# A hybrid decoder layer: the FFN's up-projection by seven half-wide products, its activations through DRAM

## The chip, the cores and the metric

One Trainium2 chip, one core. The metric is the device time of one execution in microseconds (us), as the median of several runs. TensorE (PE) multiplies; VectorE (DVE), ScalarE (ACT) and GpSimd (POOL) do the elementwise work; SyncE (SP) issues the DMAs. On-chip memory (SBUF) has 128 partitions; products are accumulated in PSUM, in banks of 512 float32 columns.

## The reference

One layer (width 2048, 512 tokens, FFN width 5632) of a decoder with two parallel mixers, then an FFN:

```python
h = rms_norm(x, mix_norm_g)
p = h @ w_in                                  # split into a_val, a_gate, q, k, v, z, b, a
out_a = conformer_conv_group(a_val, a_gate, ...)
out_b = gated_deltanet_group(q, k, v, z, b, a, ...)
x = x + concat([out_a, out_b]) @ w_out        # 2048 x 2048
h = rms_norm(x, ffn_norm_g)
gate, up = split(h @ w_up, 2)                 # w_up 2048 x 11264
gate = causal_depthwise_conv(gate, ffn_conv_w) + ffn_conv_b     # width 3
x = x + (silu(gate) * up) @ w_down            # 5632 x 2048
return rms_norm(x, final_norm_g)
```

Everything is float32. The change lies in the last five lines.

## The kernel before

Everything is held transposed: channels in the 128 partitions, the 512 tokens along the free axis. A product is cut into output tiles of 128 channels; a tile needs one step per block of 128 input channels, called k here. TensorE multiplies a rounded float32 format, so both factors are split into a high and a low part and a step is three matmuls (`mm3`, line 470): high weights by high input, high weights by low input, low weights by high input, each 128x128 weights by 512 tokens into one bank. Each of the three loads its weights anew.

`mtile` (line 476) makes one output tile and `plan_all` (line 518) lists the weights in the order of use. `load_next` (line 438) brings them by SP's queue in tiles `wraw` of 1024 columns, three of them in flight; `split_piece` (line 448) makes pieces of 512 columns (four k): `whi` by a cast on ACT, `wlo` by a subtraction on DVE.

Order of the program: input projection with the two mixers between its tiles (operands `xgh`, `xgl`, 32 tiles of the pool that `A`, line 323, draws from); first half of the output projection (`obh`, `obl`), conformer's pointwise product (`yh`, `yl`, giving `ah`, `al`), second half of the output projection, whose result `x2` stays in SBUF and is split into `h2h`, `h2l` (16 pairs). Two pools hold these 16 pairs: `H2` (line 1245) puts the first 22 tiles (k 0 to 10) into `late`, on the left, and the last 10 (k 11 to 15) into `late2`, at the right end of the partition.

The FFN runs in four chunks of 11 of its 44 tiles. `ffn_tile` (line 1263) makes a gate tile by 16 k, times `rstd2` (the RMS factor of each token, made beside the first tile), the width-3 convolution, SiLU, times `rstd2` again; an up tile by 16 k, the product of the two, and its split into `acth`, `actl`. After each chunk `down` (line 1281) adds 16 tiles of 11 k each to `x2`. The last two tiles of the last chunk are made in token halves of 256 (`half_tiles`, line 494), so that the final norm of the first half runs beside the second.

A planner (`Flow`) writes every engine's order while the program is recorded: it keeps a clock per engine by assumed costs and places the elementwise steps between the matmuls. All instructions are issued by one helper, so they all stand under line 94; one goes by the tiles' names.

Of the kernel before, what the change touches and what calls it, by code (L numbers as in the profile page):

```python
# [31 lines left out]
CHUNKS = 4  # L32
FC = NF // CHUNKS
EPS = 1e-6
# [6 lines left out]
H2_LEFT = 22  # L41
SPLIT_TILES = 2
# [30 lines left out]
class Engine:  # L73
    """Emits an engine's instructions and keeps the engine's clock by their cost."""
# [24 lines left out]
class Flow:  # L99
    """Sets every engine's instruction order: steps of the dependent chains between the bulk products."""  # L100
# [37 lines left out]
    def key(self, ap):  # L138
        n = ap.tensor.name
        return n if not n.startswith(("scr_d", "scr_n", "scr_o", "scr_y", "x2")) else (n, ap.offset)  # L140

    def account(self, eng, op, out, ins, kw):
# [148 lines left out]
def S(*aps):  # L291
# [5 lines left out]
    "y1", "e1", "d2p", "y2p", "e2",  # L297
# [4 lines left out]
def tile_trunk(ctx: ExitStack, tc: tile.TileContext, xT, w_k, w_ba, w_m, pw, w_out, w_up, w_down, par_d, cst_d, out):  # L302
# [6 lines left out]
    apool = ctx.enter_context(tc.tile_pool(name="acts", bufs=1))  # L309
    cctx, gctx = ExitStack(), ExitStack()  # L310
# [12 lines left out]
    def A(name, dt=F32R):  # L323
        return fl.tile(apool, [P, T], dt, "a", 32, nm(name))
# [27 lines left out]
    def alloc(tag, name, shape):  # L352
        fl.live[tag] += 1
        if tag == "misc":
            t = misc(name)
        elif tag == "DE":
# [79 lines left out]
    nsplit = [0, 0]  # L436

    def load_next():
        i = len(raws)
        if i < len(plan):  # L440
# [7 lines left out]
    def split_piece():  # L448
        i, o = nsplit
        if i >= len(plan):  # L450
            return
        n, step = plan[i][1:]
        w = min(step, n - o)
        src = raws[i][:, o : o + w]
        if i >= len(plan) - 2 * SPLIT_TILES:
            hi, lo = L("whi", F32R, "h2", H2_LEFT), L("wlo", F32R, "h2", H2_LEFT)
# [19 lines left out]
    def mtile(xs, release=False):  # L476
# [3 lines left out]
        while k < n:  # L480
            hi, lo = pieces.popleft()
            step = split_piece()
            for j in range(min(4, n - k, 8 - k % 8)):
                sl = blk(j)
# [3 lines left out]
                if release:  # L488
                    fl.live["a"] -= 2
# [4 lines left out]
    def half_tiles(xs, tiles, kept, half):  # L494
        ts = slice(half * 256, (half + 1) * 256)
        n = len(xs)
        for m in range(tiles):
            ps = acc()
            for k in range(n):
# [5 lines left out]
                hi, lo = kept[m * 3 + k // 4]  # L505
# [12 lines left out]
    def plan_all():  # L518
# [4 lines left out]
        for m in range(KT):  # L523
# [3 lines left out]
        for m in range(KT):  # L527
            plan_tile(w_out[m][:, 1024:2048], 1024)
        for f in range(NF):
            plan_tile(w_up[2 * f], D)  # L530
            plan_tile(w_up[2 * f + 1], D)
            if f % FC == 0 and f:
                for m in range(KT):
                    plan_tile(w_down[f // FC - 1, m], FC * P)
        for m in range(KT):
            plan_tile(w_down[CHUNKS - 1, m], FC * P)

    def split_scaled(src, g, name, alloc):
        hi = alloc(name + "h", F32R)
        lo = alloc(name + "l", F32R)  # L540
# [4 lines left out]
    def split_plain(src, name):  # L545
        hi = A(name + "h")
        lo = A(name + "l")
# [45 lines left out]
    scr_o = dram.tile([NH, P, T], F32, name="scr_o")  # L593
    scr_s, scr_t, scr_e = [dram.tile([NH * NB, P, 32], F32, name=n) for n in ("scr_s", "scr_t", "scr_e")]
# [11 lines left out]
    plan_all()  # L606
    xts = []
# [29 lines left out]
    for k in range(KT):  # L637
# [4 lines left out]
        hi, lo = split_scaled(xs, mix_g[:, k : k + 1], "xg", A)  # L642
# [501 lines left out]
    def z_task(h, ps, scan_ev):  # L1144
# [13 lines left out]
        while fl.live["a"] > 2 * KT - 2 or (h > 0 and not z_ev[h - 1].done):  # L1158
# [10 lines left out]
    fl.live["a"] = 2 * KT  # L1169

    def in_tile():
        left[0] -= 1
        return mtile(xg, left[0] == 0)
# [31 lines left out]
    late = ctx.enter_context(tc.tile_pool(name="late", bufs=1, reuse_waits="tile"))  # L1205

    def L(name, dt=F32, tag="lt", bufs=4):
        return fl.tile(late, [P, T], dt, tag, bufs, nm(name))

# [11 lines left out]
    x2, x2g = [], []  # L1221
    for m in range(KT):
        if m % 4 == 0:
            x2g.append(late.tile([P, 4, T], F32, tag="x2", bufs=KT // 4, name=nm("x2")))
        t = x2g[m // 4][:, m % 4, :]
# [4 lines left out]
        x2.append(t)  # L1230
    fl.drain(y_ev)
    ahl = []
    for m in range(NC):
# [6 lines left out]
        ahl.append((hi, lo))  # L1240
    cctx.close()
# [166 lines left out]
```

## Time and profile before

| | us |
|---|---|
| median of 3 runs | 2234.42 (2234.21 to 2236.41) |
| profiled execution, first to last instruction | 2233.0 |
| PE busy | 2219.0 (99%) |
| weight loads busy (beside PE) | 1832.2 (82%) |
| DVE busy | 1185.1 (53%) |
| ACT busy | 775.0 (35%) |
| DMA, mean over the span | 106 GB/s |

The profiled execution's span is 2233.0 us; the median of the runs shown lies 1.4 us above it. Matmuls are pipelined: one is shown from its start to its modelled end, which is longer than the distance to the next start, so a matmul's cost in a stream is read from the distance between starts. DVE's and ACT's instructions overlap their neighbours a little too. In a row of instructions by group the figures after the bar are the group's busy time, the mean length of one, and the idle time of that engine just before them, with what ended it.

### The profile page before, as it was taken

The numbers are of one execution on the slowest core, as the hardware profiler recorded it, in microseconds if no ns is written. First come the engines' busy times: TensorE is split into PE (matmuls) and PEld (weight loads), VectorE is DVE, ScalarE is ACT, GpSimd is POOL, SyncE is SP. The second block draws the span as 40 slices with busy tenths as digits, with TensorE's granted clock in tenths as the row PEclk, the third lists the DMA queues.
The fourth block names the chain that finished last, engine by engine and source line by source line (L and its number), as shares of the span: only waits on it lengthen the run. The fifth ranks groups of instructions, "written<-read, shape, count | busy, mean of one in ns | idle before, by whom it ended". The sixth has DMA issues, their size and how long they took to land.

```text
span 2233.0 us, 26443 instructions
## 1 busy us (share of the span) xinstructions
PE 2219.0 (99%) x10172; PEld 1832.2 (82%) x10172; DVE 1185.1 (53%) x2037; ACT 775.0 (35%) x1336; POOL 59.5 (3%) x59
## 2 busy tenths in 40 slices
PE   9999999999999999999999999999999999999997
PEld 7888888888888888888888888888888888888887
DVE  6899778888735544444334444334444333444444
ACT  5633554344323433322222323222233222233332
POOL 0310100000000000000000000000000000000000
PEclk9999999999999999999999999999999999999999
DMA  5352423233532222222332222332232233222223
GB/s 193 99 165 95 123 95 117 95 114 129 180 122 95 95 95 95 95 94 93 95 101 101 97 99 85 98 99 96 94 100 89 97 101 105 95 95 95 93 92 118
DMA packets 99438, 236.28 MB, mean 106 GB/s; under 512 B 21360, under 2 KB 42224, under 8 KB 99312
## 3 DMA queue, kind: packets, MB, share of 16 engines
q1 hardware_dynamic: 99168, 234.59, 31.8%
q8 instruction: 79, 1.29, 0.2%
q14 instruction: 47, 0.39, 0.1%
q10 hardware_dynamic: 144, 0.01, 0.0%
HBM read 220.41 MB, written 14.16 MB: 105 GB/s over the span
## 4 chain that ended last, share of the span: by engine, by line
PE 99%; issue 0%; DVE 0%; DMA 0%; SPq 0%; ACT 0%; POOLq 0%; POOL 0%; DVEq 0%
PE acc L94 94%; PE tr L94 1%; PE e L94 1%; PE pv L94 0%; PE ba L94 0%; PE po L94 0%; PE y L94 0%; PE psn L94 0%; PE pk L94 0%; PE pq L94 0%; DVE x L94 0%; PE y2p L94 0%; DMA wraw<-in_w_k_dram 0%; PE dec L94 0%; PE qk L94 0%
## 5 line engine op out<-in xcount | busy, mean ns | idle before, releaser
L94 DVE TENSOR_TENSOR wlo<-wraw,whi 128x512 fp32r<-128x512 f32 (+1 forms) x788 | 527.4, 678 | 557.5 <-ACT whi L94 551.6
L94 ACT CAST whi<-wraw 128x512 fp32r<-128x512 f32 (+1 forms) x788 | 473.2, 608 | 830.0 <-PE acc L94 784.8
L94 PE MATMUL acc<-h2h,whi 128*128 128x512 f32 x1408 | 551.3, 392 | 0.0
L94 PE MATMUL acc<-h2l,whi 128*128 128x512 f32 x1408 | 550.7, 391 | 0.0
L94 PE MATMUL acc<-h2h,wlo 128*128 128x512 f32 x1408 | 550.6, 391 | 0.0
L94 PEld LDWEIGHTS acc<-h2h,wlo 128*128 128x128 f32 x1408 | 264.3, 188 | 58.6
L94 PEld LDWEIGHTS acc<-h2h,whi 128*128 128x128 f32 x1408 | 264.3, 188 | 58.2
L94 PEld LDWEIGHTS acc<-h2l,whi 128*128 128x128 f32 x1408 | 264.3, 188 | 58.1
L94 PE MATMUL acc<-acth,whi 128*128 128x512 f32 (+1 forms) x726 | 277.9, 383 | 0.0
L94 PE MATMUL acc<-actl,whi 128*128 128x512 f32 (+1 forms) x726 | 277.8, 383 | 0.0
L94 PE MATMUL acc<-acth,wlo 128*128 128x512 f32 (+1 forms) x726 | 277.7, 383 | 0.0
L94 PE MATMUL acc<-xgh,whi 128*128 128x512 f32 x640 | 260.3, 407 | 0.7 <-ACT xgh L94 0.7
L94 PE MATMUL acc<-xgh,wlo 128*128 128x512 f32 x640 | 250.3, 391 | 0.0
L94 PE MATMUL acc<-xgl,whi 128*128 128x512 f32 x640 | 249.8, 390 | 0.3 <-DVE xgl L94 0.3
L94 DVE SCALAR_TENSOR_TENSOR cacc<-u,par,cacc 128x501 f32<-128x501 f32 (+24 forms) x240 | 170.6, 733 | 1.0
L94 PEld LDWEIGHTS acc<-acth,wlo 128*128 128x128 f32 x726 | 136.4, 188 | 26.7
L94 PEld LDWEIGHTS acc<-acth,whi 128*128 128x128 f32 x726 | 136.4, 188 | 26.7
L94 PEld LDWEIGHTS acc<-actl,whi 128*128 128x128 f32 x726 | 136.4, 188 | 26.6
L94 PEld LDWEIGHTS acc<-xgh,wlo 128*128 128x128 f32 x640 | 120.1, 188 | 26.2
L94 PEld LDWEIGHTS acc<-xgh,whi 128*128 128x128 f32 x640 | 120.4, 188 | 24.0 <-ACT xgh L94 1.6
L94 PEld LDWEIGHTS acc<-xgl,whi 128*128 128x128 f32 x640 | 120.5, 188 | 23.1 <-DVE xgl L94 0.9
L94 DVE TENSOR_TENSOR x<-x,acc 128x512 f32<-128x512 f32 (+1 forms) x98 | 66.3, 676 | 112.9 <-PE acc L94 111.1
(211 smaller groups left out, 1681.6 us busy)
## 6 DMA issues: line engine op xcount, KB each, us to landing
wraw<-in_w_up_dram SPq DMA_DIRECT2D x176, 512.0 KB, 3.7
wraw<-in_w_m_dram SPq DMA_DIRECT2D x74, 512.0 KB, 3.8
wraw<-in_w_down_dram SPq DMA_DIRECT2D x64, 512.0 KB, 3.5
wraw<-in_w_out_dram SPq DMA_DIRECT2D x32, 512.0 KB, 3.8
wraw<-in_w_down_dram SPq DMA_DIRECT2D x64, 192.0 KB, 2.3
x<-in_xT_dram SPq DMA_DIRECT2D x32, 256.0 KB, 4.3
wraw<-in_pw_dram SPq DMA_DIRECT2D x8, 512.0 KB, 3.6
out_dram<-x SPq DMA_DIRECT2D x6, 512.0 KB, 3.0
```

Source lines behind the costliest of these rows:

```text
L94: return f(**kw) if not args else f(out, *args, **{k: v for k, v in kw.items() if k != "out"})
```

## The change

Four parts.

**Up-projection.** For each of the 44 FFN tiles the gate rows and the up rows of `w_up`, each cut into two halves of 8 k (a11, a12 for the gate, a21, a22 for up), and the input, cut into the same halves of k and two halves of 256 tokens, form a 2x2 by 2x2 block product. It is made by seven products (Strassen's, in Winograd's form) in place of eight: 7 products x 8 k x 3 matmuls of 256 columns, into halves of four banks `bx`, `by`, `bz`, `bv`. The input's block sums are made once (`operands`) into `XT` and `XB`, on the left. The weights' sums are four DVE instructions of 1024 columns per tile (`combine`); the outputs are put together by `up_out`.

**Two phases.** All 44 activation tiles are made first and written to DRAM (`scr_a`); the layer's x goes through DRAM too (`scr_x`). Then the tiles come back (`act_loads`) and are split (`act_split`) into pairs `dh`, `dl`.

**Down-projection.** Two chunks of 22: 32 tiles of 22 k in place of 64 of 11. The `rstd2` factor of the up half is applied to the down tile (`down_add`). One tile, not two, is made in token halves.

**Pools.** The operands of `A` go into two pools of 16 tiles on the right side, `acts1` opened first (the right end), which hold `xgh`/`xgl` of k 0 to 7, then `obh`/`obl`, then `ah`/`al`; and `acts2`. The planner's cost of a matmul is now (columns + 32) / 2400 us.

```diff
-CHUNKS = 4
+CHUNKS = 2
-H2_LEFT = 22
-SPLIT_TILES = 2
+KH = KT // 2
+PAIRS = [m for j in range(KH) for m in (j, j + KH)]
+D_PRE, D_LEFT, D_RIGHT = 8, 38, 24
+SPLIT_TILES = 1
...
-                    rate = 1
-                dur = max(cols * rate / 2400.0, floor) + 0.0025
+                    rate, floor = 1, (cols + 32) / 2400.0
+                dur = max(cols * rate / 2400.0, floor) + (0.0025 if rate > 1 else 0.0)
...
+    apools = [
+        c.enter_context(tc.tile_pool(name=n, bufs=1, side="right", reuse_waits="tile"))
+        for c, n in ((actx, "acts1"), (a2ctx, "acts2"))]
...
+        ACT.copy(out=xt[:, :, 0:HT], in_=v2(d))
+        yield S(xt)
+        V.tensor_tensor(out=xt[:, :, HT:T], in0=v2(d), in1=xt[:, :, 0:HT].bitcast(F32), op=ALU.subtract)
...
+        SP.dma_start(scr_x[m], t)
+        total = add_square(t, total, S2)
+        if i % 2:
+            op_ev.append(fl.spawn(operands(i // 2, xvs[i - 1], t)))
     rstd2 = rstd_tile("rstd2_bc")
+    fl.drain(op_ev)
     fl.spawn(rms_stats(total, rstd2))
...
+                (a11, start, None), (a22, None, lambda: combine(a22, a21, a22, ALU.add)),
+                (a12, lambda: combine(a21, a11, a21), None), (a22, None, s2),
+                (a21, lambda: combine(a12, a12, a22), lambda: load(f + 1, 12)),
+                (a22, None, None if f else lambda: load(1, 22)), (a12, None, None)]
...
+    def up_out(f, s1, bx, by, bz, bv, ev2, ev3, ev4):
+        yield [ev2]
+        yield S(bv)
+        g = U("g", 2, 2 * T)
+        V.tensor_tensor(out=g[:, 0:HT], in0=s1, in1=bv[:, 0:HT], op=ALU.add)
...
+        V.tensor_tensor(out=s2, in0=s1, in1=bx[:, HT:T], op=ALU.add)
...
+        V.tensor_tensor(out=v2(u), in0=s2.unsqueeze(1).to_broadcast([P, 2, HT]), in1=v2(by), op=ALU.add)
+        V.tensor_tensor(out=g[:, T + HT :], in0=u[:, HT:T], in1=by[:, 0:HT], op=ALU.add)
...
+        V.tensor_tensor(out=g[:, HT : T + HT], in0=u, in1=bz, op=ALU.add)
...
-        V.tensor_tensor(out=a, in0=a, in1=rstd2, op=ALU.mult)
-        ps = mtile(h2)
-        V.tensor_tensor(out=a, in0=a, in1=ps, op=ALU.mult)
-        free(ps)
-        return split_plain(a, "act")
+        yield S(a)
+        V.tensor_tensor(out=a, in0=a, in1=g[:, T:], op=ALU.mult)
+        yield S(a)
+        SP.dma_start(scr_a[f], a)
...
+    def act_split(f, hi, lo):
+        yield S(lo)
+        ACT.copy(out=hi, in_=lo.bitcast(F32))
+        yield S(hi)
+        V.tensor_tensor(out=lo, in0=lo.bitcast(F32), in1=hi.bitcast(F32), op=ALU.subtract)
...
+            for k in range(KH):
+                if k % 4 == 0:
+                    hi, lo = pieces.popleft()
+                    step = refill(3 if f == NF - 1 and n > 3 else 6)
+                sl = blk(k % 4)
+                mm3(
+                    b[:, c : c + HT], hi[:, sl], lo[:, sl], x[k][:, 0:HT], x[k][:, HT:T],
+                    k == 0, k == KH - 1)
...
+    def down_add(m, ps, ts):
+        t = L("dt")
+        V.tensor_tensor(out=t[:, ts], in0=ps, in1=rstd2[:, ts], op=ALU.mult)
+        V.tensor_tensor(out=x2[m][:, ts], in0=x2[m][:, ts], in1=t[:, ts], op=ALU.add)
```

The order of the instructions moves at three places. A row gives the operation, the tile written, the tiles read and the shape of what is written; "x2" marks two alike in a row.

On PE, inside an up tile, before: a k of three matmuls over all 512 tokens.

```order
L94 MATMUL acc_7499<-h2h_6550,whi_7463 128x512
L94 MATMUL acc_7499<-h2l_6551,whi_7463 128x512
L94 MATMUL acc_7499<-h2h_6550,wlo_7464 128x512
L94 MATMUL acc_7499<-h2h_6593,whi_7463 128x512
L94 MATMUL acc_7499<-h2l_6594,whi_7463 128x512
```

And now, inside the first of the seven products of a tile (`xb` holds the high and the low half-wide operand of one k, so the two by `whi` read alike):

```order
L97 MATMUL bx_10059<-xb_6391,whi_9922 128x256 x2
L97 MATMUL bx_10059<-xb_6391,wlo_9923 128x256
L97 MATMUL bx_10059<-xb_6392,whi_9922 128x256 x2
L97 MATMUL bx_10059<-xb_6392,wlo_9923 128x256
L97 MATMUL acc_18613<-dh_18355,whi_18488 128x512
```

The last of these rows is the first of the down phase; there the matmuls are as wide as before. The number of matmuls per k stays at three, their width is halved in the up phase, and a tile has 56 k in place of 32.

On DVE, in the middle of the up phase (`wraw`, `uraw` are the weights' blocks, `wlo`, `ulo` their low parts, `s`, `u`, `g` the output's sums):

```order
L97 TENSOR_TENSOR wraw_8533<-uraw_8402,wraw_8533 128x1024
L97 TENSOR_TENSOR s_1731_8726<-s_1706_8546,bx_8505 128x256
L97 TENSOR_TENSOR u_1734_8734<-s_1731_8726,by_8506 128x512
L97 TENSOR_TENSOR g_8624<-u_1734_8734,by_8506 128x256
L97 TENSOR_TENSOR wlo_8698<-uraw_8577,whi_8697 128x512
L97 TENSOR_TENSOR uraw_8402<-wraw_8404,uraw_8402 128x1024
L97 TENSOR_TENSOR ulo_8729<-uraw_8577,uhi_8728 128x512
L97 TENSOR_TENSOR g_8624<-u_1734_8734,bz_8507 128x512
L97 TENSOR_TENSOR fg_8772<-g_8624,rstd_bc 128x512
L97 TENSOR_TENSOR wlo_8749<-wraw_8533,whi_8748 128x512
```

Before, DVE had in a tile's 32 k eight `wlo`, the chain of `fg`, `fa` and `actl`, and nothing of 1024 columns; now it has 14 low parts, four block sums of 1024 and nine instructions of `up_out` (two of them the convolution's).

On SP, where the up phase hands over to the down phase (`dl` is the tile that an activation is loaded into):

```order
L97 DMA scr_a<-fa_18404 128x512
L97 DMA wraw_18578<-in_w_down_dram 128x1024
L97 DMA x_3331_18606<-scr_x 128x512 x3
L97 DMA dl_18621<-scr_a 128x512
L97 DMA dl_18624<-scr_a 128x512
L97 DMA dl_18627<-scr_a 128x512
```

Four pairs (f 0 to 3) are loaded during the last up tile; behind the rows shown stand 19 loads of 256 KB in a row, for f 4 to 22, then the next `wraw`, then twelve more loads. Before, SP had only weights to bring in this part of the program.

## Rows read from the trace of the kernel before

**Rows 1.** The page: busy time by engine; the chain that ended last, by engine.
```profile
PE 2219.0 (99%) x10172; PEld 1832.2 (82%) x10172; DVE 1185.1 (53%) x2037; ACT 775.0 (35%) x1336; POOL 59.5 (3%) x59
PE 99%; issue 0%; DVE 0%; DMA 0%; SPq 0%; ACT 0%; POOLq 0%; POOL 0%; DVEq 0%
```
**Rows 2.** Groups by form, the up-projection's weight loads: busy us, mean ns | idle before.
```profile
L94 PEld LDWEIGHTS acc<-h2l,whi 128*128 128x128 f32 x1408 | 264.3, 188 | 58.1
L94 PEld LDWEIGHTS acc<-h2h,whi 128*128 128x128 f32 x1408 | 264.3, 188 | 58.2
L94 PEld LDWEIGHTS acc<-h2h,wlo 128*128 128x128 f32 x1408 | 264.3, 188 | 58.6
```
**Rows 3.** Timeline of PE, down-projection, 512 wide (start us, length): first and last of 37.
```profile
2193.43 0.39 PE L94 MATMUL acc<-acth,wlo 128*128 128x512 f32 x1
...
2201.59 0.39 PE L94 MATMUL acc<-acth,wlo 128*128 128x512 f32 x1
```
**Rows 4.** Timeline of PE, token halves, 256 wide: first and last of 81.
```profile
2201.82 0.28 PE L94 MATMUL acc<-acth,whi 128*128 128x256 f32 x1
...
2211.41 0.28 PE L94 MATMUL acc<-acth,wlo 128*128 128x256 f32 x1
```
**Rows 5.** Timeline of the weight loads in the same stretch.
```profile
2201.82 0.19 PEld L94 LDWEIGHTS acc<-actl,whi 128*128 128x128 f32 x1
2201.94 0.19 PEld L94 LDWEIGHTS acc<-acth,wlo 128*128 128x128 f32 x1
```
**Rows 6.** Timeline of PE, one up tile: k 0, k 11, next tile's k 0.
```profile
990.04 0.39 PE L94 MATMUL acc<-h2h,whi 128*128 128x512 f32 x1
...
997.54 0.40 PE L94 MATMUL acc<-h2h,whi 128*128 128x512 f32 x1
...
1001.04 0.39 PE L94 MATMUL acc<-h2h,whi 128*128 128x512 f32 x1
```
**Rows 7.** Windows: PE, PEld, DVE, ACT, POOL busy (instructions), PEclk, DMA share, GB/s.
```profile
0.00:56.00 56.00, 53.81 (x234) 41.65 (x235) 34.91 (x63) 32.61 (x63) 2.96 (x8) 1.00 0.54 192
770.00:1030.00 260.00, 260.00 (x1144) 213.29 (x1143) 113.64 (x168) 80.53 (x132) 1.40 (x1) 1.00 0.27 93
```
**Rows 8.** Groups by form on DVE: subtraction for a low part, convolution, 256 columns.
```profile
L94 DVE TENSOR_TENSOR wlo<-wraw,whi 128x512 fp32r<-128x512 f32 x708 | 483.0, 691 | 430.4 <-ACT whi L94 424.4
L94 DVE SCALAR_TENSOR_TENSOR fa<-fg,par,fa 128x511 f32<-128x511 f32 x44 | 33.0, 751 | 39.0 <-ACT fa L94 39.0
L94 DVE TENSOR_TENSOR x<-x,statb 128x256 f32<-128x256 f32 x32 | 10.9, 415 | 1.1 <-PE statb L94 1.1
```
**Rows 9.** Timeline of DVE while it is dense: instructions behind one another.
```profile
301.53 0.69 DVE L94 TENSOR_TENSOR wlo<-wraw,whi 128x512 fp32r<-128x512 f32 x1
302.13 0.68 DVE L94 TENSOR_REDUCE so<-osq 128x4 f32<-128x512 f32 x1
...
305.16 1.36 DVE L94 SCALAR_TENSOR_TENSOR cacc<-u,par,cacc 128x482 f32<-128x482 f32 x2
```
**Rows 10.** Groups by form on ACT.
```profile
L94 ACT CAST whi<-wraw 128x512 fp32r<-128x512 f32 x708 | 432.2, 619 | 689.1 <-PE acc L94 647.3 <-ACT whi L94 27.9 <-DVE wlo L94 6.2
L94 ACT ACTIVATE fa<-fg,par 128x512 f32<-128x512 f32 x44 | 35.9, 817 | 136.5 <-DVE fg L94 136.5
L94 ACT ACTIVATE h2h<-x,par 128x512 fp32r<-128x512 f32 x16 | 11.6, 725 | 48.1 <-DVE x L94 48.1
```
**Rows 11.** Timeline, the chain of one gate tile: idle before, and what ended it.
```profile
782.82 1.54 DVE L94 SCALAR_TENSOR_TENSOR fa<-fg,par,fa 128x511 f32<-128x511 f32 x2 [0.89 <-ACT fa L94]
784.45 0.63 ACT L94 ACTIVATE fa<-fa 128x512 f32<-128x512 f32 x1 [1.66 <-DVE fa L94]
```
**Rows 12.** DMA issues: count, KB each, median us from issue to landing.
```profile
wraw<-in_w_up_dram SPq DMA_DIRECT2D x176, 512.0 KB, 3.7
yr<-scr_y SPq DMA_DIRECT2D x8, 256.0 KB, 3.7
scr_y<-y SPq DMA_DIRECT2D x8, 256.0 KB, 2.2
```

More of the change, by code (lines that the diff above doesn't have):

```diff
@@ L451, in split_piece @@
             return
+        if i == up_at + 2:
+            have = len(pieces)
+            for _ in up:
+                if len(pieces) > have:
+                    return
+                yield
+            nsplit[:] = [i + 1, 0]
+            i, o = nsplit
         n, step = plan[i][1:]
@@ L483, in mtile @@
             for j in range(min(4, n - k, 8 - k % 8)):
+                if xs[k] is None:
+                    fl.idle(lambda: xs[k] is not None)
                 sl = blk(j)
@@ L1157, in z_task @@
         free(ot)
-        while fl.live["a"] > 2 * KT - 2 or (h > 0 and not z_ev[h - 1].done):
+        while fl.live["a"] > KT - 2 or (h > 0 and not z_ev[h - 1].done):
             yield 0.2
@@ L1252, in tile_trunk, with load_xv, S2 @@
+    xvs = []
+    def load_xv():
+        if len(xvs) < KT:
+            fl.idle(lambda: fl.live["xv"] < 6)
+            fl.live["xv"] += 1
+            xvs.append(fl.tile(tpool, [P, T], F32, "xv", 6, nm("xv")))
+            SP.dma_start(xvs[-1], scr_x[PAIRS[len(xvs) - 1]])
+    def S2(name):
+        pool, bufs = (xpool, 1) if name == "sqsum" else (tpool, 2)
+        return fl.tile(pool, [P, T], F32, name, bufs, nm(name))
+    load_xv()
     total = None
-    for m in range(KT):
+    op_ev = []
@@ L1288, in tile_trunk, with DT @@
-    acts = {}
-    for f in range(NF):
-        acts[f] = ffn_tile(f)
-        c = f // FC
-        if f % FC == 0 and c > 0:
-            for m in down(c - 1, [acts[i] for i in range((c - 1) * FC, c * FC)], KT):
-                pass
-    last = [acts[i] for i in range((CHUNKS - 1) * FC, NF)]
+        yield S(a)
+        V.tensor_tensor(out=a, in0=a, in1=g[:, T:], op=ALU.mult)
+        yield S(a)
+        SP.dma_start(scr_a[f], a)
+    dhl = [None] * NF
+    def DT(name):
+        for pool, n in dpools:
+            if fl.live[id(pool)] < n:
+                fl.live[id(pool)] += 1
+                t = fl.tile(pool, [P, T], F32R, "d", n, nm(name))
+                owner[t.tensor.name] = id(pool)
+                return t
@@ new lines, in d_room, with act_loads @@
+    def d_room():
+        return sum(n - fl.live[id(pool)] for pool, n in dpools)
+    def act_split(f, hi, lo):
[3 more added lines that the diff above has]
+        V.tensor_tensor(out=lo, in0=lo.bitcast(F32), in1=hi.bitcast(F32), op=ALU.subtract)
+        dhl[f] = (hi, lo)
+    def act_loads(fs):
+        for f in fs:
+            while d_room() < 2:
+                yield 0.2
+            yield [out_ev[f]]
+            yield S(scr_a[f])
+            hi, lo = DT("dh"), DT("dl")
+            SP.dma_start(lo.bitcast(F32), scr_a[f])
+            fl.spawn(act_split(f, hi, lo))
```

292 lines of the change are left out of this document (229 added, 63 removed).

## The prediction

> **What bounds the kernel now.** I read the page first: TensorE is busy for 99% of the span, and the chain that ended last is 99% TensorE with no share for any other engine [rows 1]. So nothing hides TensorE's time and nothing waits visibly for DVE, ACT or a DMA; the time is the number of matmuls times the distance at which they start. [...] Then I read distances. In the down-projection 36 distances of 512-wide matmuls take 2201.59 - 2193.43 = 8.16 us, 0.2267 us each [rows 3]. In the token halves at the end 80 distances of 256-wide ones take 9.59 us, 0.1199 us each [rows 4]: more than half of the wide one, since both hold the same 13 ns beyond their columns (2 x 0.1199 - 0.2267). The weight loads there start every 0.12 us while each is shown as 0.19 us long [rows 5], so they overlap one another and the matmuls. The up-projection's 4224 matmuls take, from the loads' busy and idle time, 3 x 264.3 + 58.1 + 58.2 + 58.6 = 967.8 us [rows 2], 0.2291 each, a little over the down-projection's. The reason is in one tile: k 0 to 10 take 7.50 us for 33 matmuls, 0.2273 each, k 11 to 15, whose operands lie in late2 at the right end, take 3.50 us for 15, 0.2333 each [rows 6].
>
> **The change, part by part.**
>
> *The seven products.* 44 tiles x 7 products x 8 k x 3 = 7392 matmuls of 256 columns, all with operands on the left. At 0.1199 us [rows 4] this is 886.3 us against 967.8: **-81.5 us**. The columns alone fall by an eighth, 113 us; the 13 ns, paid 3168 times more, take back 41; late2's excess, 10, goes. [...]
>
> *Operands at the right end.* acts1 is the first pool on the right and 32 KB deep, so it covers the 20 KB where late2 lay. In it lie now half of the input projection's pairs (960 matmuls), all of obh/obl (384) and ah/al (384); of the down-projection's 44 pairs I count 9 at the right end (432). A matmul there costs 0.2333 - 0.2267 = 6.6 ns more, or 7.9 ns if the whole excess of the tile, 11.00 - 48 x 0.2267 = 0.12 us, is put on its 15 [rows 6]. 2160 x 6.6 to 7.9 ns = 14.3 to 17.1; I take **+15.7 us**. No row shows that the place is the cause rather than the pool, so the lower bound is 0.
>
> *VectorE in the up phase.* A tile gives TensorE 168 x 0.1199 = 20.14 us. DVE has in it 14 low parts, four block sums of 1024 columns, and in up_out three instructions of 256, four of 512 and two of the convolution. Listed lengths are 0.691, 0.415 and 0.751 us [rows 8]; behind one another a 512-column one starts 0.60 us after the one before it, and two convolution-like ones take 1.36 us together, not 1.47 [rows 9], so about 0.09 us of each is covered by its neighbour. 1024 columns are in no row; 512 to 256 differ by 0.276 us, which makes 0.691 + 2 x 0.276 = 1.24 listed, 1.15 in a row; below 1.07 or above 1.38 (twice 0.691) it can hardly lie. The sum: 14 x 0.605 + 4 x 1.15 + 3 x 0.33 + 4 x 0.605 + 2 x 0.66 = 17.8 us, 88% of the tile. The products can run up to six pieces (8.6 us) behind DVE, so short waits in DVE's order are absorbed. I add **+3 us** for 44 tiles, with bounds 0 and 25 (0.57 us a tile, what a DVE 2.9 us over its sum would cost). ACT has 14 casts of 0.619 and 1.9 us more [rows 10, 11], 10.6 of 20.14: it hides. The DMA moves 2.36 MB per tile, 117 GB/s, where 93 are moved now and 192 were moved in the first window [rows 7]: it hides too.
>
> *Into the up phase.* The last pair of x needs, after the last output-projection matmul, on ACT and DVE in turn: add 0.69, square 0.62, two scalings 0.73, casts and differences of 256 to 1024 columns; 7.9 us in all from [rows 8, 10]. The first product can start at once and needs the pair as its eighth k; the second needs the block differences, which are last. Behind them DVE still has, in order, a low part, two sums of 1024 and the low parts of a12 before the third product can go. I place the third product's end at 13.4 us where 8.6 would be unhindered: **+5 us** (2 to 9).
>
> *Into the down phase.* k 4 of the first down tile needs an activation that is loaded only when the last products release their operands' space. A 256 KB read back from DRAM lands 3.7 us after its issue and a write 2.2 us [rows 12]. In DVE's order the last tile's convolution and product stand ahead of the splits, to about 5 us after the last up matmul; then 18 splits and 5 weight pieces at 0.605 us follow, 13.9 us, and k 21 runs at about 20 us, not 15.0. The loads are as slow: 192 GB/s at a share of 0.54 [rows 7] is 356 at most, 0.74 us for each of 22 loads in a row, and the next weights queue behind 31. **+8 us** (4 to 16).
>
> *The rest.* One more DVE instruction of 256 columns, 0.42 us [rows 8], in the chain after the last matmul: **+0.4**. Rows of x2 through DRAM, the second instruction per down tile (0.69 us in 15) and the larger chunks lie beside TensorE's work in a phase where DVE has half of its time free [rows 7]; without that cover they would be 32 x 0.69 = 22 us. The planner's new matmul cost reorders the first 620 us a little; TensorE was full there and stays so: 0 +- 4.
>
> **The sum:** -81.5 + 15.7 + 3 + 5 + 8 + 0.4 = -49.4; 2233.0 - 49.4 = 2183.6 us of span. The median of the runs lies 1.4 us above the span: **2185 us**.
>
> **The rivals.**
>
> *VectorE becomes the bound (the slower one).* If its instructions did not overlap, the listed lengths would count: 14 x 0.691 + 4 x 1.24 + 3 x 0.415 + 4 x 0.69 + 2 x 0.751 = 20.1 us, the whole of TensorE's 20.14, and every wait in its order would come on top. Two waits like the 0.89 us before the convolution [rows 11] make 21.9 us a tile, 964 us, nothing saved, and the other terms (+29.1) remain: about 2260 us. It decides from 21.3 us of DVE per tile on (938.7 / 44): there the change is worth nothing. [...] Half of it (20.6 to 21.3 us, 2205 to 2235) is as likely as the whole.
>
> *A half-wide pass is not held at 0.120 us.* It is shown for 10 us, and would have to hold for 886. From 0.127 us (938.7 / 7392) on nothing is gained; if the weight loads of 0.19 us [rows 5] came one by one it would be 1390 us, some 2690 in all. Rows 5 show them overlapping, and nothing there depends on the length of the stretch.
>
> *The right end costs nothing* (late2's excess has another cause): the 15.7 us fall away, 2170 us.
>
> That the change doesn't do what it says is excluded by the order of the built program: seven groups of eight k, 256 wide.
>
> **How the numbers follow.** A measurement of this kernel tells about 0.2%, 4.5 us, from no change. My forecast (2172 to 2205) has 0.74; the free right end 0.12; VectorE as bound 0.06 in half (2205 to 2235) and 0.05 in full; the slow pass 0.03. Range 2164 to 2212: low, the free right end and small hand-overs; high, the hand-overs' upper bounds and a third of the DVE bound of 25. Faster 0.91, the same 0.03, slower 0.06.
>
> **What would show it.** Right: starts of bx, by, bz, bv matmuls 0.120 us apart; the first bx to the last bz about 895 us; DVE near 88% of that stretch; xgh matmuls of k 0 to 7 about 7 ns farther apart than the rest; gaps of a few us at both hand-overs. Wrong: PE waiting for wlo or ulo all through the up phase, DVE full; distances over 0.125 with no wait; or a gap of over 16 us where the down phase begins.

## The result, and the profile after

The changed kernel takes **2182.98 us** (median of four runs, 2180.41 to 2183.37); the kernel before, run beside it, 2234.84 (2234.21 to 2236.41). The ratio is 0.9765, 95% interval 0.9751 to 0.9779: 2.3% faster. The forecast was 2185 us, 2164 to 2212. The profiled execution of the changed kernel has a span of 2178.6 us, against 2233.0: 54.4 us less, where the sum said 49.4 (the profiled execution is the fastest of the four; the medians are 51.9 apart).

The page, busy time by engine and the chain that ended last, answers to [rows 1]:

```profile
PE 2156.8 (99%) x13340; PEld 1924.6 (88%) x13340; DVE 1626.3 (75%) x2684; ACT 954.9 (44%) x1664; POOL 60.9 (3%) x59
...
PE 98%; DVE 1%; issue 0%; DMA 0%; ACT 0%; SPq 0%; POOL 0%; POOLq 0%; DVEq 0%; ACTq 0%
```

TensorE is still the bound; VectorE has risen from 53% to 75%. To see where the time went I cut the span at the first matmul of each stage. The timeline of PE (start us, length), kernel before, at the start of the output projection and of the FFN:

```profile
548.72 0.39 PE L94 MATMUL acc<-obh,whi 128*128 128x512 f32 x1
...
768.22 0.39 PE L94 MATMUL acc<-h2h,whi 128*128 128x512 f32 x1
```

And after: the output projection's start, the first up tile, the second, the third, the last of 44, the down phase, its token halves:

```profile
557.23 0.39 PE L97 MATMUL acc<-obh,whi 128*128 128x512 f32 x1
...
781.48 0.40 PE L97 MATMUL bx<-xb,whi 128*128 128x256 f32 x2
...
811.08 0.40 PE L97 MATMUL bx<-xb,whi 128*128 128x256 f32 x2
...
831.05 0.40 PE L97 MATMUL bx<-xb,whi 128*128 128x256 f32 x2
...
1649.96 0.40 PE L97 MATMUL bx<-xb,whi 128*128 128x256 f32 x2
...
1669.93 0.39 PE L97 MATMUL acc<-dh,whi 128*128 128x512 f32 x1
...
2146.76 0.28 PE L97 MATMUL acc<-dh,whi 128*128 128x256 f32 x1
```

Three readings. The FFN starts 781.48 - 768.22 = 13.3 us later than before, 8.5 of it already at the start of the output projection: the stages ahead of the FFN, which the change was not about, have become slower. A tile in the steady up phase takes (1649.96 - 831.05) / 41 = 19.97 us, 118.9 ns per matmul; the first one takes 811.08 - 781.48 = 29.6, 9.6 more. And from the start of the down phase to its token halves it is 476.8 us, where 31 tiles x 66 matmuls x 0.2267 us are 463.8.

What has become slower there are the wide (512-column) matmuls, in the output projection as well as in the input projection. The timeline of PE in the output projection's second half, first and last of 43 matmuls:

```profile
699.91 0.39 PE L97 MATMUL acc<-ah,whi 128*128 128x512 f32 x1
...
709.67 0.39 PE L97 MATMUL acc<-ah,whi 128*128 128x512 f32 x1
```

9.76 us / 42 = 232.4 ns, where the left-hand operands of before had 226.7 [rows 3]. Now windows (columns as in [rows 7]): the steady up phase, then pieces of the first up tile, then one of the hand-over to the down phase:

```profile
800.00:1660.00 860.00, 860.00 (x7236) 860.00 (x7235) 795.01 (x1162) 434.54 (x733) 0.00 (x0) 1.00 0.38 120
...
782.00:784.00 2.00, 0.19 (x2) 0.19 (x2) 1.30 (x3) 1.60 (x3) 0.00 (x0) 1.00 0.41 145
...
786.00:787.00 1.00, 1.00 (x7) 1.00 (x6) 1.00 (x3) 0.00 (x0) 0.00 (x0) 0.50 1.04 389
...
789.00:791.00 2.00, 0.42 (x2) 0.12 (x1) 1.97 (x4) 0.73 (x2) 1.38 (x1) 0.50 0.00 0
...
1677.00:1678.00 1.00, 1.00 (x2) 0.56 (x3) 1.00 (x2) 0.83 (x2) 0.00 (x0) 0.50 1.06 395
```

In the steady up phase TensorE never stops and VectorE is busy for 795.0 of 860 us, 92%: 18.5 us of each 19.97. In the first tile TensorE stands still twice, and between the stops the granted clock is 0.50: a k of three matmuls takes 0.64 us there in place of 0.36. The clock is at 0.50 again a few us into the down phase. What TensorE waited for, by the waits of PE (us in total, times, longest):

```profile
PE acc L97 <- ACT dh L97: 4.0, 1, 4.0
PE statb L97 <- POOL rstd L97: 2.7, 2, 1.6
PE stat L97 <- DVE sqsum L97: 1.8, 1, 1.8
```

So the first tile's stops are not for weights or operands, as I had placed them, but for the sixteen little matmuls of the RMS statistics: 1.8 us for the sum of squares (`sqsum`), 1.6 for its inverse root (`rstd`) from GpSimd (the rest of the 2.7 is in the tail). Of the first tile's 9.6 us these two waits are 3.4, the sixteen matmuls themselves 3.2, and most of the remaining 3.0 is the lower clock: nine k, six between the stops and three behind the second, take 5.9 us in place of 3.2. At the hand-over it is one wait for the first reloaded activation. The timeline around it (idle before, and what ended it, in brackets):

```profile
1669.50 0.33 SPq L97 DMA_DIRECT2D wraw<-in_w_down_dram  x1
1669.92 1.33 SPq L97 DMA_DIRECT2D x<-scr_x  x3
...
1671.35 10.62 SPq L97 DMA_DIRECT2D dl<-scr_a  x17
...
1676.23 1.19 ACT L97 CAST dh<-dl 128x512 fp32r<-128x512 f32 x2 [1.55 <-DMA dl<-scr_a]
...
1676.90 0.80 PE L97 MATMUL acc<-dh,whi 128*128 128x512 f32 x1 [4.03 <-ACT dh L97]
```

The first `dl` is issued behind a weight load, which waits 3.9 us until VectorE has read its buffer for a `wlo`, and behind three loads of x2, and lands 4.8 us later. Last, three of VectorE's new instructions in the up phase (groups by form; busy us, mean ns, idle before):

```profile
L97 DVE TENSOR_TENSOR ulo<-wraw,uhi 128x512 fp32r<-128x512 f32 x176 | 120.7, 686 | 31.4 <-ACT uhi L97 31.4
...
L97 DVE TENSOR_TENSOR wraw<-uraw,wraw 128x1024 f32<-128x1024 f32 x44 | 53.9, 1224 | 1.5
...
L97 DVE TENSOR_TENSOR s<-s,bx 128x256 f32<-128x256 f32 x43 | 18.1, 421 | 15.8 <-PE bx L97 15.8
```

A sum of 1024 columns takes 1.22 us (I had worked out 1.24; the 1.07 that I named as a lower limit was worked out from no row). Most of VectorE's idle time is two short waits in a tile, 0.7 us (31.4 over 43 tiles) and 0.4 us (15.8 over 43).

### The profile page after: what moved, and what is told of

It reads as the page before. It is cut to its first block, busy times and chain, and to the rows that moved or that the text cites. A ratio compares the mean times of both kernels' runs of the same rounds, so it can differ in the third digit from the quotient of the medians.

```text
span 2178.6 us, 34210 instructions
## 1 busy us (share of the span) xinstructions
PE 2156.8 (99%) x13340; PEld 1924.6 (88%) x13340; DVE 1626.3 (75%) x2684; ACT 954.9 (44%) x1664; POOL 60.9 (3%) x59
## 4 chain that ended last, share of the span: by engine, by line
PE 98%; DVE 1%; issue 0%; DMA 0%; ACT 0%; SPq 0%; POOL 0%; POOLq 0%; DVEq 0%; ACTq 0%
PE acc L97 53%; PE bz L97 12%; PE by L97 12%; PE bx L97 11%; PE bv L97 6%; PE tr L97 1%; PE e L97 1%; PE pv L97 0%; PE ba L97 0%; PE po L97 0%; PE y L97 0%; PE psn L97 0%; PE pk L97 0%; PE pq L97 0%; DVE x L97 0%
## 5 line engine op out<-in xcount | busy, mean ns | idle before, releaser
L97 PE MATMUL acc<-dh,whi 128*128 128x512 f32 (+1 forms) x726 | 280.8, 387 | 4.0 <-ACT dh L97 4.0
L97 PE MATMUL acc<-dl,whi 128*128 128x512 f32 (+1 forms) x726 | 280.6, 386 | 0.0
L97 PE MATMUL acc<-dh,wlo 128*128 128x512 f32 (+1 forms) x726 | 280.4, 386 | 0.0
L97 DVE SCALAR_TENSOR_TENSOR cacc<-u,par,cacc 128x495 f32<-128x495 f32 (+22 forms) x240 | 172.5, 737 | 1.8 <-ACT cacc L97 0.4
L97 PEld LDWEIGHTS acc<-dh,whi 128*128 128x128 f32 x726 | 136.9, 189 | 33.2 <-ACT dh L97 4.5
L97 PEld LDWEIGHTS acc<-dl,whi 128*128 128x128 f32 x726 | 136.9, 189 | 29.3 <-DVE dl L97 0.4
L97 PEld LDWEIGHTS acc<-dh,wlo 128*128 128x128 f32 x726 | 136.9, 189 | 28.8
L97 DVE TENSOR_TENSOR ulo<-wraw,uhi 128x512 fp32r<-128x512 f32 x176 | 120.7, 686 | 31.4 <-ACT uhi L97 31.4
L97 PE MATMUL by<-xt,whi 128*128 128x256 f32 x704 | 129.6, 282 | 0.0
L97 PE MATMUL by<-xt,uhi 128*128 128x256 f32 x704 | 129.0, 280 | 0.0
```

Of the source, the lines that this page charges most:

```text
L97: return f(**kw) if not args else f(out, *args, **{k: v for k, v in kw.items() if k != "out"})
```

## The experiments

**1. Why are the right-hand operands slow?** In the changed kernel the weights and operands on the left start 0x060 bytes behind a multiple of 2 KB, and those on the right at 0x7E0; in the kernel before all wide operands were at 0x060 but `late2`, at 0x7E0. (The traces hold no addresses. These starts are stated, as in the expectations; what the runs test is what a shift of 1920 bytes does.) So "right end" and "this offset" can be told apart by an empty strip of 1920 bytes:

```diff
+    padpool = ctx.enter_context(tc.tile_pool(name="pad", bufs=1, side="right"))
+    padpool.tile([P, 480], F32, name="pad")
```

> The changed kernel with 1920 bytes per partition left empty ahead of everything on the right side, so that every operand there starts at offset 0x060 within 2 KB, as on the left, where it started at 0x7E0; order, sizes and side stay as they are. Theory A, the offset makes a 512-wide matmul slow: distances of xgh, obh, yh, ah and of the right-hand dh fall from 232-233 to about 227 ns, and the time falls by the 13.3 us that the part before the FFN had become longer, less what else lies in them, and 7.4 us of the down phase: 16 to 21 us, 2162 to 2167 us. Theory B, the right end of the partition or the pool makes it slow: distances stay at 232-233 and the time stays within 3 us of 2183. The up phase (888 us) stays as it is under both.

Measured: 2171.31 us (2169.43 to 2173.17), ratio to before 0.9712 (0.9696 to 0.9729). The same 42 distances as above:

```profile
689.92 0.39 PE L97 MATMUL acc<-ah,wlo 128*128 128x512 f32 x1
...
699.44 0.39 PE L97 MATMUL acc<-ah,wlo 128*128 128x512 f32 x1
```

9.52 / 42 = 226.7 ns, at the same end of the partition: theory A, it is the offset and not the place. But the gain is 12 us, not 16 to 21. The stage marks show that 10.4 us are won ahead of the FFN and 5.7 in the down phase, and that the up phase, which was to stay, lost 9. Two of its tile starts, 41 tiles apart:

```profile
822.02 0.40 PE L97 MATMUL bx<-xb,whi 128*128 128x256 f32 x2
...
1648.58 0.40 PE L97 MATMUL bx<-xb,whi 128*128 128x256 f32 x2
```

20.16 us a tile, 168 x 120.0 ns, in place of 19.97. The strip had moved `uhi` and `ulo`, half of the up phase's weights, too.

**2. The strip without the up phase.**

```diff
-    actx, a2ctx, cctx, gctx = [ExitStack() for _ in range(4)]
+    actx, a2ctx, cctx, gctx, padctx = [ExitStack() for _ in range(5)]
+    padctx.enter_context(tc.tile_pool(name="pad", bufs=1, side="right")).tile([P, 480], F32, name="pad")
...
     actx.close()
+    padctx.close()
...
         uctx.close()
+        ctx.enter_context(tc.tile_pool(name="pad2", bufs=1, side="right")).tile([P, 480], F32, name="pad2")
```

> As the kernel with 1920 bytes empty on the right, but the empty space is given up for the up phase and taken again for the down phase: the moving operands of the wide matmuls start at 0x060 (but for the first eight tiles of the down phase), while the up phase's own pool, with uhi and ulo, lies at 0x7E0 again, as in the changed kernel. In the fully shifted kernel the up phase took 897.6 us with distances of exactly 120.0 ns, in the changed one 888.3 with 112 to 124 ns, 118.9 on average. Theory W, weights read from 0x7E0 shorten the half-wide distances: the up phase takes 888 again, with the same uneven distances, and the span is 2178.6 - 10.4 (before the FFN) - 4.4 (down phase) = about 2164 us, the time about 2166. Theory N, the evenness came with something else in the shifted kernel: the up phase takes 897, the time about 2175.

Measured: 2167.04 us (2165.78 to 2168.39), 0.9696 (0.9679 to 0.9712), span 2164.4. A tile takes 19.97 us again: theory W, whose 2166 us and span of 2164 are met within 1 us. The FFN starts 11.0 us earlier than in the changed kernel (770.47), although TensorE has a stop in the output projection that the changed kernel does not have, 2.3 us for VectorE's `cacc`, a tile of the conformer's convolution.

**3. The kernel before, with its late2 shifted.** The same strip ahead of `late2`.

> The kernel before with 1920 bytes per partition left empty ahead of late2, so that k 11 to 15 of the up-projection start at 0x060 within 2 KB like k 0 to 10. By the offset (theory A) all distances of h2h and h2l are 227 ns, the up-projection's 4224 matmuls take 957.6 in place of 967.8 us, and the time falls by 8 to 11 us to about 2225. By the place at the right end (theory B): no change. Under A the change is worth 10 us less than it shows against a kernel with this repaired.

Measured: 2224.20 us in one run, span 2222.1, the distances of `h2h` and `h2l` 226.7 ns on average: theory A. Of the change's gain, then, 10 us came from leaving a bad place that a strip of 1920 bytes would have cured; with both kernels repaired it is 2224 against 2167.

**4. Weights at the other offset.** Is 0x7E0 bad in itself, or only beside weights at 0x060? First the weights of all stages go to 0x7E0, on top of experiment 2 (with three pairs of activations loaded ahead in place of four):

```diff
-D_PRE, D_LEFT, D_RIGHT = 8, 38, 24
+D_PRE, D_LEFT, D_RIGHT = 6, 38, 24
...
+    ctx.enter_context(tc.tile_pool(name="padl", bufs=1)).tile([P, 480], F32, name="padl")
     wpool = ctx.enter_context(tc.tile_pool(name="wts", bufs=1))
...
+    ctx.enter_context(tc.tile_pool(name="padm", bufs=1)).tile([P, 32], F32, name="padm")
     gpool = gctx.enter_context(tc.tile_pool(name="gdn", bufs=1))
```

> The kernel with the wide operands at 0x060 and the up phase's pool at 0x7E0, and in addition whi and wlo of all stages moved from 0x060 to 0x7E0 (three pairs of activations are loaded ahead in place of four). Theory W, a weight load from 0x7E0 is what shortens the half-wide distances: now all 24 matmuls of a product have the uneven distances that the twelve with uhi and ulo have, about 118 ns and not 118.9, 4 to 7 us less in the up phase, and wide distances may fall below 226.7 too. Theory X, it is the change from one offset to the other within a product: the distances become even, 120.0, and the up phase takes 897 us.

Measured: 2185.85 us in one run. In the up phase a tile takes 19.94 us, distances of 118.7 ns: not the even 120.0 of theory X, but theory W's gain is 1.6 us in 44 tiles, not 4 to 7. The surprise is in the wide matmuls, which are slow again although their moving operands lie at 0x060:

```profile
699.99 0.39 PE L97 MATMUL acc<-ah,whi 128*128 128x512 f32 x1
...
709.75 0.39 PE L97 MATMUL acc<-ah,whi 128*128 128x512 f32 x1
```

9.76 / 42 = 232.4 ns. So one more run, with the weights moved as above, but no strip on the right:

> The changed kernel with whi and wlo moved from 0x060 to 0x7E0 and nothing else shifted (three pairs of activations are loaded ahead in place of four): before the FFN weights and moving operands of the wide matmuls now both start at 0x7E0, in the down phase the right-hand dh are at 0x7E0 and the left-hand ones at 0x060. So far 0x060 with 0x060 gave 226.7 ns, and 0x7E0 on either side alone 232 to 233. Theory R, what counts is that weights and moving operand start at the same offset: 226.7 again before the FFN (10 us less), and in the down phase the right-hand dh are the quicker ones and the left-hand ones the slower; about 2174 us. Theory Q, any operand at 0x7E0 slows a wide matmul: 232 or more before the FFN and for the right-hand dh; 2183 to 2187 us. In the up phase both expect the even 119.0 ns of the run with weights at 0x7E0.

Measured: 2171.06 us in one run.

```profile
689.91 0.39 PE L97 MATMUL acc<-ah,whi 128*128 128x512 f32 x1
...
699.43 0.39 PE L97 MATMUL acc<-ah,whi 128*128 128x512 f32 x1
```

226.7 ns with both at 0x7E0; and in the down phase the right-hand `dh`, at 0x7E0, now have a mean distance of 226.7 ns and the left-hand ones, k by k, of 232 to 235, the reverse of the changed kernel. Theory R: a wide matmul with its own weight load takes 226.7 ns when weights and moving operand start at the same offset, 232 to 235 when one is at 0x060 and the other at 0x7E0.

For 256 columns no such rule comes out. In the up phase, whose moving operands lie at 0x060, it is 120.0 ns with all weights at 0x060 too and 118.7 with all at 0x7E0. But the token halves at the end of the down phase are 256 wide as well, and there, in the first half of the tokens, the run just shown has for right-hand operands both at 0x7E0:

```profile
2137.38 0.28 PE L97 MATMUL acc<-dh,whi 128*128 128x256 f32 x1
...
2142.37 0.28 PE L97 MATMUL acc<-dh,whi 128*128 128x256 f32 x1
```

4.99 us for 42 distances, 118.7 ns although the starts are equal. The changed kernel (weights at 0x060, operands at 0x7E0) has 118.8 there, experiment 1 (both at 0x060) 120.0, and the first run of this experiment (weights at 0x7E0, operands at 0x060) 119.9 although they differ. Other offsets weren't tried, and why any of it is so stays open: no run here shows why 512 columns take 5.7 ns in 227 more when the two starts differ.

**5. How near is VectorE to being the bound?** Two of a tile's 14 low parts, then six, are subtracted twice:

```diff
...
             V.tensor_tensor(out=lo, in0=src, in1=hi.bitcast(F32), op=ALU.subtract)
+            redo[0] = (redo[0] + 1) % 14
+            if redo[0] in (3, 10):
+                V.tensor_tensor(out=lo, in0=src, in1=hi.bitcast(F32), op=ALU.subtract)
```

> The changed kernel with 2 of the 14 low parts of each tile subtracted twice, 1.2 us more VectorE work per tile. Theory A, TensorE bounds the up phase until VectorE's sum passes 19.97 us: VectorE is busy for 18.5 us of a tile (795.0 of 860 us in the window), 19.7 with the addition, and the time rises by 0 to 6 us. Theory B, VectorE's order already costs, its waits cannot be filled: 44 x 1.2 = 53 us more, about 2236.

> The changed kernel with 6 of the 14 low parts of each tile subtracted twice, 3.6 us more VectorE work per tile. Theory A (TensorE bounds up to 19.97 us of VectorE): 18.5 + 3.6 = 22.1 us, 2.1 us over, 44 x 2.1 = 94 us more, about 2277; TensorE waits for wlo and ulo in every tile. Theory B (every instruction of VectorE counts): 44 x 3.6 = 158 us, about 2341. If VectorE had far more room than its busy time says: under 2200.

And from the other side, TensorE's work is cut below VectorE's: this kernel leaves out seven of the eight k of every tile's second product.

```diff
-                mm3(
-                    b[:, c : c + HT], hi[:, sl], lo[:, sl], x[k][:, 0:HT], x[k][:, HT:T],
-                    k == 0, k == KH - 1)
+                if n != 1 or k == 0:
+                    mm3(
+                        b[:, c : c + HT], hi[:, sl], lo[:, sl], x[k][:, 0:HT], x[k][:, HT:T],
+                        k == 0, k == KH - 1 or n == 1)
```

> The changed kernel without seven of the eight k of the second product of every tile (21 of a tile's 168 matmuls; their weights are still loaded, cast and subtracted), so that TensorE's work in a tile falls from 19.97 to 17.5 us and VectorE's, ScalarE's and the DMA's stay. The tile's time is then the floor of VectorE. My sum for it was 17.8 us: up phase 44 x 17.8 = 783 us, 105 less in all, about 2078. If the listed lengths count (20.1 us, the slower rival): no gain. From the window's busy time, 18.5: 65 less, about 2118; from the run with six additions (22.97 - 3.63 = 19.3): 28 less, about 2155.

Measured: 2180.49, 2294.69 and 2107.12 us, one run each. The windows from 800 to 1580 us, in this order (one line of each kernel):

```profile
800.00:1580.00 780.00, 780.00 (x6563) 780.00 (x6563) 767.71 (x1131) 385.53 (x663) 0.00 (x0) 1.00 0.38 120
```

```profile
800.00:1580.00 780.00, 725.53 (x5834) 714.67 (x5833) 766.59 (x1136) 330.48 (x585) 0.00 (x0) 0.97 0.34 107
```

```profile
800.00:1580.00 780.00, 768.27 (x6291) 752.55 (x6290) 770.58 (x1148) 398.61 (x726) 0.00 (x0) 1.00 0.43 131
```

With two additions VectorE is busy for 98% and TensorE still never waits: not a microsecond lost, theory A. With six, TensorE waits, in the same stretch, for `ulo`:

```profile
PE by L97 <- DVE ulo L97: 49.8, 32, 1.9
```

The time lies between both theories' numbers, nearer to A's. From the fifth on a tile takes 22.7 us, 2.7 more; I had priced a repeated subtraction at 0.60, and it took 0.72: two together are 1.41 us long, one 0.69.

```profile
1207.82 1.41 DVE L97 TENSOR_TENSOR wlo<-wraw,whi 128x512 fp32r<-128x512 f32 x2
```

The tiles say the same: (22.7 - 18.3) / 6 = 0.73, with 18.3 from the cut kernel, its tile starts 41 apart:

```profile
827.15 0.40 PE L97 MATMUL bx<-xb,whi 128*128 128x256 f32 x2
...
1576.07 0.40 PE L97 MATMUL bx<-xb,whi 128*128 128x256 f32 x2
```

748.92 / 41 = 18.27 us a tile with VectorE busy for 99%: that is VectorE's floor here. My sum said 17.8, the rival 20.1, the window of the changed kernel 18.5. TensorE's 19.97 leave it 1.7 us; the rival was that far off, and no farther. Where the 0.5 us over my sum are, VectorE's timeline in the cut kernel shows:

```profile
1214.89 0.68 DVE L97 TENSOR_TENSOR g<-u,bz 128x512 f32<-128x512 f32 x1
1215.61 0.69 DVE L97 TENSOR_TENSOR fg<-g,rstd_bc 128x512 f32<-128x512 f32 x1
1216.22 0.69 DVE L97 TENSOR_TENSOR ulo<-wraw,uhi 128x512 fp32r<-128x512 f32 x1
```

`fg`, which reads the `g` just made, starts 0.72 us behind it; `ulo`, which reads another tile, 0.61 behind `fg`. Five neighbours in a tile are 0.11 to 0.12 us farther apart like this: `u` and `g`, `g` and `fg`, the two of the convolution, and two low parts followed by a sum that writes a `wraw`. My sum had given all of them the shorter distance.

**6. The hand-over to the down phase.** First the x2 loads alone, behind the first down tile's matmuls:

```diff
         fl.idle(lambda: bool(lpool))
+        if c == 0 and m == 0:
+            load_x2_next(2)
...
-    load_x2(0)
-    load_x2(1)
...
     for m in range(KT):
-        load_x2(m + 2)
+        if m:
+            load_x2_next(1)
         down(0, m)
```

> The changed kernel with the first three loads of x2 moved from ahead of the down phase's activation loads to behind the first down tile's matmuls. Theory A, the stall of 6.8 us at the hand-over to the down phase is the loads' (the first dh waits for a dl that stands behind 768 KB of x2): the loads land 1.4 to 3.6 us sooner and the stall falls to 3 to 5.5 us, the time by 1.5 to 3.5 us. Theory B, VectorE's order sets it (the last tile's convolution and product ahead of the first split): stall and time stay within 1 us.

Measured: 2183.91 us in one run; down phase to its halves 479.5 us, 2.7 more than in the changed kernel. Theory A's gain of 1.5 to 3.5 us did not come, and theory B's unchanged stall neither. The first cast came 4.0 us after the last up matmul, not 6.4, and the wait of 4.0 us became one of 1.6: the loads did set the first wait; but further waits for `dh` and `dl` stood behind it, and x2, now late, held VectorE's queue until `wlo` was missing:

```profile
1703.57 0.50 PE L97 MATMUL acc<-dh,wlo 128*128 128x512 f32 x1 [3.68 <-DVE wlo L97]
```

Then the loads ahead of both the weights and x2, and the last tile's chain later:

```diff
         free(bz)
+        if f == NF - 1:
+            yield 6.0
...
+            hold[0] = f == NF - 1 and n >= 5
...
-    fl.spawn(act_loads(range(D_PRE // 2, NF)))
+    fl.spawn(act_loads(range(D_PRE // 2, D_PRE // 2 + 8)))
+    fl.run()
+    hold[0] = False
+    for _ in held:
+        load_next()
...
     load_x2(1)
+    fl.spawn(act_loads(range(D_PRE // 2 + 8, NF)))
```

> The changed kernel with the hand-over to the down phase put in another order: on SyncE the first eight activation loads stand ahead of the next weights and of x2, and the last tile's convolution and product come some us later. Theory A, each of the two alone hides the other (the run that moved only x2 lost at DVE what it won on the loads): with both moved, the first activation's loads no longer wait behind a weight load for VectorE, and the gaps at the hand-over fall from 6.8 us to 0 to 3, the time by 3 to 6 us. Theory B, the operands' space is what comes last (loads cannot start before the last product): the loads start no sooner, the gaps stay at 5 to 7 us and the time within 1.5 us.

Measured: 2179.37 us in one run, 475.2 to the halves, 1.7 less than in the changed kernel. Loads (timeline of SyncE) and the one larger wait (of PE):

```profile
1667.29 4.95 SPq L97 DMA_DIRECT2D dl<-scr_a  x8
...
1682.00 0.50 PE L97 MATMUL acc<-dh,whi 128*128 128x512 f32 x1 [1.98 <-ACT dh L97]
```

The eight loads now start before the last product ends (1671.0), so the operands' space was not what came last: theory B falls. The first wait is gone, but another one ends 11 us into the phase, at the ninth load, which stands behind the weights and x2 now; so theory A's 0 to 3 us of gaps did not come either: some 5 of the 6.8 are left. The first tile of the phase needs 18 loads in its 15 us; whatever was put behind others here was the next one late.

**7. The statistics later.**

```diff
         yield N(r)
+        yield hold
...
-    fl.spawn(rms_stats(total, rstd2))
+    fl.spawn(rms_stats(total, rstd2, 4.0), 4.0)
```

> The changed kernel with the FFN's RMS-statistics matmuls placed some 4 us later in TensorE's order, and the second four another 4 us behind them. Theory A, TensorE stands in these places for sqsum (VectorE) and rstd (GpSimd), not for weights or operands as I had forecast: the two waits, about 4 us together, vanish and nothing takes their place; 3 to 4.5 us less. Theory B, the third product's weights would have been late anyway: the waits move to wlo or uhi and the time stays within 1 us.

Measured: 2177.17 us in one run, 3.2 below the fastest of the changed kernel's four. Both theories have a part: the waits for `sqsum` and `rstd` are gone and three smaller ones, 0.5 and 0.9 us for `xb` and 0.8 for `wlo`, have come. The first tile takes 26.6 us, 3.0 less than in the changed kernel and still 6.6 more than a steady one. The clock is at 1.00 where it had been 0.50 (and at 0.50 later, for some three microseconds from about 791 on):

```profile
784.00:786.00 2.00, 0.96 (x6) 0.55 (x5) 2.00 (x4) 1.50 (x4) 0.00 (x0) 1.00 0.92 243
```

**8. All of it.** Experiments 2 and 7, and experiment 6 with all 18 loads of the first chunk ahead of x2.

> The repairs together: wide operands at 0x060 while uhi and ulo stay at 0x7E0 (2167.0 measured, span 2164.4), the RMS-statistics matmuls later (3 us less measured), and at the hand-over all 18 activation loads of the first chunk ahead of x2, with one weight load among them. If the gaps are independent of one another, the span is 2164.4 - 3 - (2 to 5) = 2156 to 2160 us and the time 2158 to 2162. If what is won at the hand-over is lost again at x2 or the next weights, as in the run with the other order (4.4 us of gaps came 12 us later): 2163 to 2165.

Measured: **2159.77 us** (2158.87 to 2162.06), ratio to before 0.9667 (0.9654 to 0.9680): the fastest of all here, 23 us under the change as it was, and as expected of gaps that are independent. What waits are left at the hand-over, and its clock:

```profile
PE acc L97 <- DVE dl L97: 2.6, 4, 1.0
```

```profile
1660.00:1664.00 4.00, 3.85 (x17) 2.68 (x15) 3.01 (x6) 2.59 (x6) 0.00 (x0) 1.00 1.02 392
1664.00:1666.00 2.00, 1.19 (x5) 0.63 (x5) 2.00 (x5) 2.00 (x4) 0.00 (x0) 1.00 1.05 394
```

Four short waits in place of a long one, and the clock stays at 1.00.

## Why the prediction was right, point by point

| term | forecast, us | measured, us | from |
|---|---|---|---|
| seven half-wide products | -81.5 | -89.0 | 44 x 19.97 = 878.8 against 967.8 |
| operands at the right end | +15.7 | +18.9 | FFN's start 781.48 - 768.22; down phase 476.8 - 471.2 (experiment 1) |
| waits for VectorE in the up phase | +3 | 0 | no wait from 800 to 1660 us |
| into the up phase | +5 | +9.6 | 29.6 - 20.0 |
| into the down phase | +8 | +7.4 | 476.8 - 463.8, less 5.6 of slow distances |
| tail | +0.4 | +0.7 | halves to end: 31.9 against 31.2 |
| early stages in another order | 0 | about 0 | nothing of the 13.3 us is left for it, see below |
| span | -49.4 | -54.4 | |

The measured terms add up to -52.4; the other 2 us are waits and statistics that stood in the FFN of before beside its matmuls (2201.8 - 768.2 = 1433.6 us, of which 967.8 + 463.8 are matmuls).

That the sum came within 5 us, and the time within 2, is in part luck. The products saved 7.5 us more than forecast and VectorE cost 3 less, the 2 us of before were not in the sum; the right end cost 3.2 and the way into the up phase 4.6 more, and these errors largely cancel.

- **The seven products** were the right mechanism at a slightly wrong size. A matmul of half the width still paid most of the 13 ns beyond its columns, all through the up phase: 118.9 ns against the 119.9 forecast, so about 12.1 of the 13.1 that 2 x 119.9 - 226.7 gives [rows 3, 4], an estimate. The last nanosecond hangs on the offset of `uhi` and `ulo` (experiments 1, 2).
- **The right end**: the amount lies a little above the highest value that the forecast gave it, 17.1, and it is that near by luck, for three steps of it were wrong. The cause is not the place but how the operand's start stands to that of its weights (experiments 1 and 4). The count was too low: it hit all of the input projection and `yh`, `yl` too, since `acts2` has the same offset, 2880 matmuls ahead of the FFN where I counted 1728; and 20 of the down phase's 44 pairs, not 9 (k 0 to 3 of the first chunk and 1 to 16 of the second have distances of 232 to 235), 912 wide matmuls where I counted 432. The price was too high, 6.6 to 7.9 ns: it is 4.6 in the input projection (232.7 against 228.1 in experiment 2), 5.7 to 6.0 up to the FFN and 6.4 in the down phase. 1920 x 4.6 + 960 x 5.7 ns = 14.3 us explain all of the 13.3 by which the FFN starts later. Experiment 2 wins back 11.0 of them; the stop of 2.3 us for `cacc`, which it has and the changed kernel has not, is the difference. The rival "the right end costs nothing" was wrong for this kernel, but its 2170 us is what a strip of empty bytes gives (2167 to 2171).
- **VectorE** was the step on which the sign could have turned. Its sum was 0.5 us a tile too low (17.8 against a floor of 18.3), since five neighbours in a tile start 0.11 to 0.12 us later than it had them (experiment 5); the forecast of 88% met 92%, and the shortfall was covered by the 1.7 us that TensorE leaves. That the products can run several pieces behind VectorE fits: at 98% there is not one wait. How many pieces it is, no run measured.
- **Into the up phase** is the step whose mechanism failed: 9.6 us came out, above its bound of 9. I had priced the way of the last operands and of the third product's weights; the waits for them are 0.5, 0.9 and 0.8 us when nothing else stands in the way (experiment 7). What stopped TensorE were the statistics, which the planner had put into the first product (my reading of the planner is that waiting for the operands had moved its clock; no run tests that). Their chain goes through VectorE, where `ms`, the mean square, stands behind the last operands' splits, and GpSimd. In experiment 1 the clock stayed at 1.00 between the two stops, and the first tile took no less (30.8 us): the second wait was longer by as much, since the chain ended 9.5 us after the first product's start, as in the changed kernel (791.0 - 781.5; here 780.6 - 771.1). So the slow clock between the stops cost nothing of its own there, since the chain and not TensorE set the end of the second stop. The timeline of that run:

```profile
778.94 0.15 DVE L97 TENSOR_SCALAR ms<-stat 128x4 f32<-128x4 f32 x1
779.17 1.38 POOL L97 TENSOR_TENSOR rstd<-ms,mhalf 128x4 f32<-128x4 f32 x1 [181.73 <-DVE ms L97]
...
780.61 2.08 PE L97 MATMUL statb<-cst,rstd 128*128 128x128 f32 x8 [3.91 <-POOL rstd L97]
```

- **Into the down phase** had the right size for half the reason. The loads, not the convolution on VectorE, ended last; with all 18 loads of the first chunk sooner, the waits that are left are for VectorE's `dl` (experiment 8).

## What to carry to other kernels

Read the distance between starts, in the form and for the operands that the new code will use, before trusting a count of columns: here half the width cost 119 ns and not 113, half of 226.7, and the part beyond the columns was forecast to take back 41 of the 113 us that fewer columns save. A change of pools moves offsets as well as places: here 1920 empty bytes were worth 12 to 16 us. Look at where tiles start when alike instructions differ. Where phases meet, list all that the engine has in its order, the small matmuls of statistics too: here the smallest of them waited for the longest chain, and the large ones behind them waited too.

## What was not expected of the hardware

- Two starts, 0x060 and 0x7E0, of weights and of the moving operand: 512 wide 226.7 ns if equal, 232.4 (up to 235 in the down phase) if not, whichever has which. 256 wide, in the up phase with operands at 0x060: 120.0 with all weights at 0x060, 118.9 with half of them at 0x7E0, 118.7 with all; in the first token half of the down phase 118.7 to 118.8 with the operand at 0x7E0 and 119.9 to 120.0 with it at 0x060, wherever the weights are (experiment 4).
- Behind a stop of 1.8 us the granted clock was 0.50 from about 784 us until past 794 in the changed kernel; in experiment 1 the same stop left it at 1.00, and it fell at the next, of 3.9 us. With waits of 0.5, 0.9 and 0.8 us in the first tile it was at 0.50 for some three microseconds in experiment 7 and stayed at 1.00 in experiment 8. So the length of a stop alone does not tell which level follows.
- A subtraction repeated onto the tile that it has just written started 0.72 us behind the first, not the 0.60 of unlike neighbours [rows 9], and so did `fg` behind the `g` that it reads (experiment 5).
